# Delta net: V turned by a 16-bit DMA, projections in another order, the output projection's second half in two depths

## The chip, the cores and the metric

One core of a Trainium2 chip runs the whole program. The metric is the device time of one execution in microseconds; lower is better. TensorE (PE), VectorE (DVE), ScalarE (ACT), GpSimd (POOL) and SyncE (SP, which here only issues transfers) run side by side, each through its own list of instructions in order.

## The reference

Two layers on a residual stream of 1024 tokens by 1024 channels: a gated delta net, then chunked attention, each with a gated convolutional feed-forward behind it. The change lies in the first, of 8 heads and 16 chunks of 64 tokens in the reference (the kernel solves 128 tokens at a time).

```python
def gated_deltanet(xn, w_in, conv_w, A_log, dt_bias, out_norm_w, w_out):
    proj = xn @ w_in
    qkv = jax.nn.silu(causal_dwconv(proj[..., :A_CONV_WIDTH], conv_w))
    z = ...; b_raw = ...; a_raw = ...
    q = _l2norm(q) * (A_HEAD_K ** -0.5); k = _l2norm(k); v = qkv[..., 2 * A_QK_WIDTH:]
    beta = jax.nn.sigmoid(b_raw)
    g = -jnp.exp(A_log) * jax.nn.softplus(a_raw + dt_bias)
    o = chunk_gated_delta_rule(q, k, v, beta, g)
    # S_t = exp(g_t) (I - beta_t k_t k_t^T) S_{t-1} + beta_t k_t v_t^T ; o_t = S_t^T q_t
    o = rmsnorm(o, out_norm_w) * jax.nn.silu(z)
    return o.reshape(bsz, seq, A_V_WIDTH) @ w_out

h = h + gated_deltanet(rmsnorm(h, a_norm), ...)
```

## The kernel before, in words

All is kept with channels on the 128 partitions and tokens along them. A product in full precision is three matmuls, of high and low parts (`dense`, L118 to L120): one unit is the three for one block of 128 input channels and 512 tokens, and a tile of 128 output channels and 512 tokens (a half) is eight units. Weights come as `wraw`, ScalarE makes their high part `whi`, GpSimd the low part `wlo` in four slices (L103).

In the delta net, the projections (tiles `acc`) are woven with the heads' small work by a planner, `Flow`. It keeps a clock `T` of its own and a free time per engine, takes the small items that its costs say are ready, by rank, and otherwise one more dense unit; so it writes out the order of PE, DVE and ACT. SP and POOL are ordered by the framework. A list `ORDER` says in which order the projections of K, Q and V of each head come.

A projection's two halves pass `post`: copies out on ACT, the convolution's taps on DVE, then `silu`: a Tanh on ACT and two POOL instructions (L626, L627). V is stored to DRAM as `d_v`, channels by tokens (L630). `prep` loads it for a head and half as `vv` (L761), PE turns it into the PSUM tile `pv` with four transposes (L778), and DVE multiplies it by `sk` back into `vv` (L780). `chain` then walks the chunks: PE products `pc`, DVE and ACT in turns, with `y` written by ACT (L935). `turn` and `turn_last` turn the heads' results for the output projection (L985, L1032), and `split_yt` makes high and low parts of them, `acts`.

The output projection runs tile by tile, first the eight of the first 512 tokens, then the eight of the second (`out_tile`, PSUM tiles `acco`). Each loads one weight tile and the residual as two planes of 16 bits (`xm`), which POOL and DVE weave into `xs` (L1299); DVE adds `xs` to the sum (L1305). A tile of the second half can start when all eight `acts` of that half are there:

```python
wv.dense.append((lambda: True, there("begun", *[("act", k, s) for k in range(KT)]), out_tile(m, s)))
```

The sums of squares for the next norm are gathered after each tile (L357, L359), and when a half is done its normed high and low parts `xh`, `xl` are made (L381 is a low part).

In the attention layer's key and value stage V is already turned through DRAM as 16-bit halves (`turn_halves`, L2201 to L2222, with tiles `vt`, `vu`, `vf`); a similar pair of transfers turns `x` at the start (`xm`, `d_xt`).

## Time and profile before

| | us |
|---|---|
| runs of the kernel: median | 2497.89 |
| runs: lowest, highest | 2497.13, 2501.19 |
| span of the profiled execution | 2493.3 |
| PE, DVE, ACT, POOL busy | 2466.1, 1842.5, 1442.1, 1523.0 |

The profile covers one execution, of which its page gives the span, from the first to the last instruction; what the runs have more lies around the span, and no other time of that execution is listed. A group's row reads: line, engine, operation, what it writes and reads, how often; shortest, median and longest in ns. A row of waits reads: who waited for whom, us in all, times, longest. In a row of the timeline stand the start, the length, the instruction and its count. PE's lengths overlap, so its pace is read from starts.

### The profile page before, as it was taken

How to read it: one execution, taken by the hardware profiler on the slowest of the kernel's cores; microseconds unless marked ns; L12 is line 12 of the kernel's file. 1: busy time of each engine (PE TensorE's matmuls, PEld its weight loads, DVE VectorE, ACT ScalarE, POOL GpSimd, SP SyncE). 2: the span in 40 equal slices, each digit the busy share in tenths (PEclk: the TensorE clock that was granted, in tenths of full speed). 3: DMA queues.
4: the chain of work that ended last, by engine and by line, in shares of the span. 5: the costliest groups of instructions: out<-in, count | busy, mean ns of one | idle time of the engine just before them, and what ended most of it. 6: DMA issues, size and time to landing. Idle time of an engine off the chain costs nothing.

```text
span 2493.3 us, 39279 instructions
## 1 busy us (share of the span) xinstructions
PE 2466.1 (99%) x13785; PEld 2057.0 (83%) x13785; DVE 1842.5 (74%) x2985; ACT 1442.1 (58%) x2770; POOL 1523.0 (61%) x1548
## 2 busy tenths in 40 slices
PE   8999999999999999999999999999999999999998
PEld 6888888888888888888788888888877888888877
DVE  5665874567798888888866656666589788888886
ACT  6444546474465556565555666667456565666555
POOL 3655653357357777777626454455554777778774
PEclk9999999999999999999999999999999999999999
DMA  8734435565347777777841232333444799777788
GB/s 228 188 105 118 142 110 153 156 194 163 96 108 148 150 153 151 153 144 156 183 151 55 67 80 77 81 76 95 145 114 119 184 176 180 166 169 171 152 187 224
DMA packets 383877, 353.19 MB, mean 142 GB/s; under 512 B 97600, under 2 KB 304448, under 8 KB 383680
## 3 DMA queue, kind: packets, MB, share of 16 engines
q1 hardware_dynamic: 350704, 243.46, 34.4%
q0 software_dynamic: 28224, 98.58, 22.5%
q10 hardware_dynamic: 4752, 8.65, 0.9%
q8 instruction: 108, 1.77, 0.3%
q14 instruction: 89, 0.73, 0.1%
HBM read 182.25 MB, written 156.30 MB: 136 GB/s over the span
## 4 chain that ended last, share of the span: by engine, by line
PE 81%; POOL 6%; DVE 4%; issue 4%; DMA 2%; ACT 2%; SPq 0%; ACTq 0%; POOLq 0%; DVEq 0%
PE acc L118 8%; PE pu L1448 8%; PE acc L119 8%; PE acc L120 8%; PE pu L1446 8%; PE pu L1447 8%; PE pd L1448 3%; PE pd L1446 3%; PE pd L1447 3%; POOL ul L1412 3%; PE acco L118 2%; PE acco L120 2%; PE acco L119 2%; PE ptp L2353 2%; PE poT L2399 1%
## 5 line engine op out<-in xcount | busy, mean ns | idle before, releaser
L1412 POOL TENSOR_TENSOR ul<-r,uh 128x512 fp32r<-128x512 f32 x266 | 430.4, 1638 | 258.3 <-ACT uh L1434 253.5
L118 PE MATMUL acc<-xh,whi 128*128 128x512 f32 x896 | 369.3, 413 | 0.5 <-ACT xh L1094 0.5
L119 PE MATMUL acc<-xl,whi 128*128 128x512 f32 x896 | 352.1, 393 | 0.4 <-POOL xl L381 0.3
L120 PE MATMUL acc<-xh,wlo 128*128 128x512 f32 x896 | 351.3, 392 | 0.0
L103 POOL TENSOR_TENSOR wlo<-wraw,whi 128x256 fp32r<-128x256 f32 (+1 forms) x326 | 237.0, 758 | 107.8 <-ACT whi L101 105.3
L1434 ACT CAST uh<-r 128x512 fp32r<-128x512 f32 x289 | 177.1, 623 | 183.3 <-DVE r L1412 148.8
L1448 PE MATMUL pu<-xh,ul 128*128 128x512 f32 x524 | 204.4, 390 | 0.7 <-POOL ul L1412 0.7
L1446 PE MATMUL pu<-xh,uh 128*128 128x512 f32 x524 | 204.4, 390 | 0.7 <-ACT keep L1575 0.7
L1802 ACT COPY stage<-pd 128x1024 f32<-128x1024 f32 x180 | 175.3, 1014 | 49.7 <-PE pd L1448 48.8
L1447 PE MATMUL pu<-xl,uh 128*128 128x512 f32 x524 | 203.9, 389 | 0.0
L120 PEld LDWEIGHTS acc<-xh,wlo 128*128 128x128 f32 x896 | 168.5, 188 | 37.1
L2308 POOL TENSOR_SCALAR sS<-sS,st 128x640 f32<-128x640 f32 (+4 forms) x128 | 87.6, 691 | 178.4 <-DVE st L2306 168.2
L119 PEld LDWEIGHTS acc<-xl,whi 128*128 128x128 f32 x896 | 169.3, 189 | 28.4 <-POOL xl L381 2.5
L118 PEld LDWEIGHTS acc<-xh,whi 128*128 128x128 f32 x896 | 169.1, 189 | 27.5 <-ACT xh L1094 0.9
L1412 POOL TENSOR_TENSOR dl<-a,dh 128x512 fp32r<-128x512 f32 x90 | 153.3, 1703 | 47.4 <-ACT dh L1434 37.2
L1541 DVE SCALAR_TENSOR_TENSOR gate<-gpre,colt,gate 128x1023 f32<-128x1023 f32 (+2 forms) x92 | 176.5, 1919 | 2.5 <-ACT gate L1538 1.8
L1541 DVE SCALAR_TENSOR_TENSOR val<-vpre,colt,val 128x1023 f32<-128x1023 f32 x88 | 149.2, 1696 | 29.3 <-ACT val L1538 29.3
L2298 DVE CUSTOM_DVE_ANT_0 sS<-sc,bt 128x640 f32<-128x640 f32 (+4 forms) x128 | 84.1, 657 | 111.4 <-PE sc L2294 75.9
L1412 DVE TENSOR_TENSOR r<-r,r 128x512 f32<-128x512 f32 x160 | 130.3, 814 | 32.8 <-POOL ul L1412 31.7
L1412 DVE TENSOR_TENSOR el<-val,eh 128x512 fp32r<-128x512 f32 x90 | 85.4, 949 | 43.2 <-ACT eh L1434 43.2
L1448 PEld LDWEIGHTS pu<-xh,ul 128*128 128x128 f32 x524 | 98.4, 188 | 22.8 <-POOL ul L1412 1.4
L1446 PEld LDWEIGHTS pu<-xh,uh 128*128 128x128 f32 x524 | 98.4, 188 | 21.1 <-ACT keep L1575 1.1
(428 smaller groups left out, 7197.9 us busy)
## 6 DMA issues: line engine op xcount, KB each, us to landing
r<-in_f_w_up_dram SPq DMA_DIRECT2D x176, 256.0 KB, 4.5
d_r<-stage POOLq DMA_DIRECT2D x78, 512.0 KB, 8.1
d_c<-stage POOLq DMA_DIRECT2D x70, 512.0 KB, 8.4
a<-in_f_w_down_dram SPq DMA_DIRECT2D x72, 256.0 KB, 2.9
wraw<-in_a_w_in_dram SPq DMA_DIRECT2D x32, 512.0 KB, 4.5
d_e<-stage POOLq DMA_DIRECT2D x32, 512.0 KB, 8.3
wraw<-in_a_w_out_dram SPq DMA_DIRECT2D x16, 512.0 KB, 4.1
d_r<-h ACTq DMA_DIRECT2D x32, 256.0 KB, 2.8
```

Of the source, the lines that this page charges most:

```text
L103: nc.gpsimd.tensor_tensor(lo[:, c], raw[:, c], hi[:, c].bitcast(F32), op=ALU.subtract)
L118: mm(ps, hi[:, kw, wcol : wcol + P], rh[k][s], start=st, stop=False)
L119: mm(ps, hi[:, kw, wcol : wcol + P], rl[k][s], start=False, stop=False)
L120: mm(ps, lo[:, kw, wcol : wcol + P], rh[k][s], start=False, stop=sp)
L1412: tt = lambda eng, o, a, b, op: eng.tensor_tensor(o, a, b, op=op)
L1434: copy(hi, src)
L1446: mm(ps, w[0][:, cw], x[0], start=first, stop=False, skip_group_check=True)
L1447: mm(ps, w[0][:, cw], x[1], start=False, stop=False, skip_group_check=True)
L1448: mm(ps, w[1][:, cw], x[0], start=False, stop=last, skip_group_check=True)
L1541: nc.vector.scalar_tensor_tensor(t_[:, a:c1], p_[:, a - step : c1 - step], w[:, 2 - step : 3 - step], t_[:, a:c1], op0=ALU.mult, op1=ALU.add)
L1802: nc.scalar.copy(t_, ps)
L2308: nc.gpsimd.tensor_scalar(S, S, st[:, 3:4], 1.0, op0=ALU.mult, op1=ALU.mult)
```

## The change

Four things change; the pools' tags for a few small tiles (`tri`, `ba`, `gr`, `nck`, `eg`) change with them, to make room.

1. V is turned by DMA. Behind `silu`, ACT copies V into two planes of 16-bit halves (`cast`, L641), SP stores them in pieces of 128 tokens, and `prep` loads a head and half with a transposing DMA into `vh` (one buffer). ACT copies one plane and POOL the other into `vv` (L788, L789), and DVE multiplies `vv` by `sk` in place. PE no longer takes part.
2. `ORDER` has other places for some of the projections.
3. The second half of the output projection is computed in two passes: `out_deep` takes two output tiles at once, first over input blocks 0 to 3 for all eight tiles, then over blocks 4 to 7. The first pass adds the residual into `h`, the second adds its sum to `h`. A weight load is 4 blocks by 256 columns instead of 8 by 128.
4. The first pass may start when `acts` 0 to 3 of the second half are there, the second when 4 to 7 are.

```diff
-    d_v = [[dram.tile([P, HALF], F32, name=f"d_v{k}_{s}") for s in range(2)] for k in range(KT)]
+    d_v = [[dram.tile([SEQ, P], mybir.dt.uint16, name=f"d_v{k}_{s}") for s in range(2)] for k in range(KT)]
...
+        planes = lambda t_: t_.bitcast(U16).rearrange("p (h t) -> p h t", h=2)
+        woven = lambda t_: t_.bitcast(U16).rearrange("p (t h) -> p h t", h=2)
...
                     t = wv.on("G", 2.0, wv.on("A", 0.66)) + 0.6
+                    if key[0] == "v":
+                        wv.later(t - 0.6, lambda: cast(th))
+                        return
...
+                def cast(th):
+                    nc.scalar.copy(planes(th), woven(d))
+                    nc.sync.dma_start(out=store[s].rearrange("(h b c) t -> c h b t", h=2, b=4), in_=th.bitcast(U16).rearrange("p (h b t) -> p h b t", h=2, b=4))
+                    wv.mark((key[0], key[1], s), wv.on("A", 1.02) + 3.0)
...
-            vv = dp.tile([P, 4, P], F32, name="vv", tag="vv", bufs=4)
-            nc.sync.dma_start(out=vv.rearrange("p c t -> p (c t)"), in_=d_v[hd][s])
+            vh = dq.tile([P, 2, HALF], U16, name="vh", tag="vh")
+            nc.sync.dma_start(out=vh.rearrange("p h t -> p (h t)"), in_=d_v[hd][s], transpose=True)
             t1_ = wv.T + 5.0
...
-            slot = yield from wv.bank()
-            pv = paux.tile([P, HALF], F32, name="pv", tag="pa")
-            for c in range(4):
-                nc.tensor.transpose(pv[:, cs(c)], vv[:, c], ident)
-            wv.pe(4, 0.11)
-            nc.vector.tensor_tensor(vv, pv.rearrange("p (c t) -> p c t", c=4), sk[...].broadcast_to([P, 4, P]), op=ALU.mult)
-            slot[0] = t2_ = wv.on("D", 1.18)
+            vv = dp.tile([P, 4, P], F32, name="vv", tag="vv", bufs=4)
+            w_ = woven(vv.rearrange("p c t -> p (c t)"))
+            nc.scalar.copy(w_[:, 0], vh[:, 0])
+            nc.gpsimd.tensor_copy(w_[:, 1], vh[:, 1])
+            yield max(wv.on("A", 0.78), wv.on("G", 0.93)) - wv.slack
+            nc.vector.tensor_tensor(vv, vv, sk[...].broadcast_to([P, 4, P]), op=ALU.mult)
+            t2_ = wv.on("D", 0.7)
...
+        def out_deep(ms, k0):
+            raw = wp.tile([P, 4, 2 * P], F32, name="wraw", tag="wraw", bufs=2)
+            nc.sync.dma_start(out=raw, in_=a_w_out[k0 * P : (k0 + 4) * P, ms[0] * P : (ms[1] + 1) * P].rearrange("(k p) m -> p k m", p=P))
+            xms = [out_x(m, 1) for m in ms if k0 == 0]
+            yield
+            wt = split_w(raw, [P, 4, 2 * P])
+            wv.on("G", 2.75, wv.on("A", 1.0))
+            yield 4
+            for n, m in enumerate(ms):
+                if k0 == 0:
+                    ps, xs = out_begin(xms[n])
+                else:
+                    ps, xs = pacc.tile([P, HALF], F32, name="acco", tag="acc", bufs=3), h[m][:, hs(1)]
+                for k in range(4):
+                    dense(ps, wt, n * P, *acts, [(k, k0 + k)], 1, first=k == 0, last=k == 3)
+                    if k < 3:
+                        yield
+                if k0 == 0:
+                    nc.vector.tensor_tensor(h[m][:, hs(1)], ps, xs, op=ALU.add)
+                    wv.on("D", 0.64)
+                else:
+                    out_end(m, 1, ps, xs)
+                yield
...
-        ORDER = [... "k2 k0 k1 k3 q2 q0 q1 k5 k4 q3 v0 v1 k6 v2 v3 k7 q4 q5 q6 q7 v5 v4 v6 v7".split()]
+        ORDER = [... "k2 k0 k1 k3 k5 k4 q2 q0 q1 v0 v1 k6 k7 q3 v2 v3 q4 q5 v5 v4 q6 q7 v6 v7".split()]
...
-            for s in range(2):
-                for m in range(KT):
-                    wv.dense.append((lambda: True, there("begun", *[("act", k, s) for k in range(KT)]), out_tile(m, s)))
+            for m in range(KT):
+                wv.dense.append((lambda: True, there("begun", *[("act", k, 0) for k in range(KT)]), out_tile(m, 0)))
+            for k0 in (0, 4):
+                for m in range(0, KT, 2):
+                    wv.dense.append((lambda: True, there(*[("act", k, 1) for k in range(k0, k0 + 4)]), out_deep((m, m + 1), k0)))
```

`out_begin` and `out_end` are the first and last parts of the old `out_tile`: the weaving of `xs`, and the add with the step of the next norm behind it.

The order of PE around the first `prep` of a head (`pqk` is its product of K and Q), before:

```order
L767 MATMUL pqk<-kq 128x128 x4
L118 MATMUL acc<-xh_1_245,whi 128x512
L119 MATMUL acc<-xl_1_246,whi 128x512
L120 MATMUL acc<-xh_1_245,wlo 128x512
L778 MATMUL pv<-ident,vv 128x128 x4
L118 MATMUL acc<-xh_1_249,whi 128x512
```

and now:

```order
L862 MATMUL pm<-D,X 32x32 x32
L778 MATMUL pqk<-kq 128x128 x4
L118 MATMUL acc<-xh_0_253,whi 128x512
L119 MATMUL acc<-xl_0_254,whi 128x512
L120 MATMUL acc<-xh_0_253,wlo 128x512
L118 MATMUL acc<-xh_0_257,whi 128x512
```

The group `pv` is gone from between the units; `pqk` is now L778.

ACT where the first V projections are copied out (L625 or L628 is the Tanh), before:

```order
L610 ACTIVATE u<-acc,colt 128x512
L612 ACTIVATE u<-acc,colt 128x3
L625 ACTIVATE th<-u 128x512
L847 COPY X<-pm 128x256
L689 ACTIVATE E<-E,ngc 128x128 x4
```

and now:

```order
L628 ACTIVATE th<-u 128x512
L641 COPY th<-u 128x1024
L858 COPY X<-pm 128x256
L101 CAST whi<-wraw 128x1024
L641 COPY th<-u 128x1024
L628 ACTIVATE th<-u 128x512
L788 COPY vv<-vh 128x512
```

Copies into planes (L641) and out of `vh` (L788) now stand in ACT's list between a merge's copy `X`, a weight split and the next Tanh.

POOL in the second half of the output projection (`wlo` is a weight split of four slices, `xl` a low part of the normed first half), before:

```order
L1299 COPY xs<-xm 128x512
L103 TENSOR_TENSOR wlo<-wraw,whi 128x256 x4
L1299 COPY xs<-xm 128x512
L381 TENSOR_TENSOR xl_0_7200<-h_1_6584,xh_0_7199 128x512
L103 TENSOR_TENSOR wlo<-wraw,whi 128x256 x4
L1299 COPY xs<-xm 128x512
```

and now:

```order
L1073 TENSOR_TENSOR xl_1_6541<-vv,xh_1_6540 128x512
L1310 COPY xs<-xm 128x512
L103 TENSOR_TENSOR wlo<-wraw,whi 128x256 x4
L1310 COPY xs<-xm 128x512 x2
L103 TENSOR_TENSOR wlo<-wraw,whi 128x256 x4
L1310 COPY xs<-xm 128x512
L381 TENSOR_TENSOR xl_0_7209<-h_1_6608,xh_0_7208 128x512
L1310 COPY xs<-xm 128x512
L381 TENSOR_TENSOR xl_0_7213<-h_3_6610,xh_0_7212 128x512
L103 TENSOR_TENSOR wlo<-wraw,whi 128x256 x4
```

Between two splits stood one copy `xs`, and stand now two, while the first pass runs.

More of the change, by code (lines that the diff above doesn't have):

```diff
@@ L510, in trunk_kernel @@
         dp = ph.enter_context(tc.tile_pool(name="dp", bufs=1, **SB))
-        tri = dp.tile([P, P], F32, name="tri")
+        tri = dp.tile([P, P], F32, name="tri", tag="y0", bufs=2)
         nc.gpsimd.affine_select(out=tri, in_=ones, pattern=[[1, P]], compare_op=ALU.is_ge, fill=0.0, base=0, channel_multiplier=-1)
@@ L522, in trunk_kernel @@
         dq = early_dp.enter_context(tc.tile_pool(name="dq", bufs=1, side="right", **SB))
-        ba = dp.tile([P, 8, 16], F32, name="ba")
+        ba = dp.tile([P, 8, 16], F32, name="ba", tag="S0", bufs=2)
         def gt(name):
@@ L529, in trunk_kernel @@
         beta, gg, t1, t2 = gt("beta"), gt("gg"), gt("t1"), gt("t2")
-        eg, neg_eg, ekd, dec = gt("eg"), gt("neg_eg"), gt("ekd"), gt("dec")
+        neg_eg, ekd, dec = gt("neg_eg"), gt("ekd"), gt("dec")
         gc = dp.tile([P, 2, 8, 8], F32, name="gc")
         gcum, gtot = gc[:, 0], gc[:, 1]
-        gr = dp.tile([64, P], F32, name="gr")
+        gr = dp.tile([P, P], F32, name="gr", tag="S1", bufs=2)[0:64]
         ngc = gt("ngc")
@@ L547, in rsqrt @@
                 nc.vector.scalar_tensor_tensor(y, w, 1.5, y, op0=ALU.add, op1=ALU.mult)
-        ssk, ssq, sk, ck, nck = gt("ssk"), gt("ssq"), gt("sk"), gt("ck"), gt("nck")
+        ssk, ssq, sk, ck, nck = gt("ssk"), gt("ssq"), gt("sk"), gt("ck"), t1
         soo, ff, rr = gg, gt("ff"), gt("rr")
@@ L553, in trunk_kernel @@
         tiles = [0, 0]
+        U16 = mybir.dt.uint16
+        planes = lambda t_: t_.bitcast(U16).rearrange("p (h t) -> p h t", h=2)
+        woven = lambda t_: t_.bitcast(U16).rearrange("p (t h) -> p h t", h=2)
         def units(s, wt, post):
@@ L1153, in gates @@
             nc.sync.dma_start(out=d_g.rearrange("c j t -> (c j) t"), in_=gr)
-            nc.scalar.activation(eg, gcum, AF.Exp)
+            nc.scalar.activation(neg_eg, gcum, AF.Exp)
             nc.scalar.activation(dec, gtot, AF.Exp)
@@ L1157, in gates @@
             nc.scalar.activation(ekd, t2, AF.Exp)
-            nc.vector.tensor_scalar(neg_eg, eg, -1.0, None, op0=ALU.mult)
+            nc.vector.tensor_scalar(neg_eg, neg_eg, -1.0, None, op0=ALU.mult)
             er = dp.tile([64, P], F32, name="er", tag="junk", bufs=1)
@@ L1274, in trunk_kernel @@
         its = {}
-        U16 = mybir.dt.uint16
         d_xt = dram.tile([2 * SEQ, SEQ], U16, name="d_xt")
@@ L1283, in turn_halves, with out_raw, out_x, out_begin @@
             yield wv.T + 6.0
-        def out_tile(m, s):
-            shape = [P, KT, P]
-            raw = wp.tile(shape, F32, name="wraw", tag="wraw", bufs=2)
+        def out_raw(m, s):
+            raw = wp.tile([P, KT, P], F32, name="wraw", tag="wraw", bufs=2)
             nc.sync.dma_start(out=raw, in_=a_w_out[:, m * P : (m + 1) * P].rearrange("(k p) m -> p k m", p=P))
+            return raw, out_x(m, s)
+        def out_x(m, s):
             xm = dp.tile([P, 2, HALF], U16, name="xm", tag="xm", bufs=2)
             nc.sync.dma_start(out=xm, in_=d_xt.rearrange("(c h) t -> c h t", h=2)[m * P : (m + 1) * P, :, hs(s)])
-            yield
-            wt = split_tile(raw)
-            yield 4
+            return xm
+        def out_begin(xm):
             ps = pacc.tile([P, HALF], F32, name="acco", tag="acc", bufs=3)
@@ L1300, in out_tile, with out_end @@
             wv.on("G", 0.60), wv.on("D", 0.6)
-            for k in range(KT):
-                dense(ps, wt, 0, *acts, FULL[k : k + 1], s, first=k == 0, last=k == KT - 1)
-                if k < KT - 1:
-                    yield
+            return ps, xs
+        def out_end(m, s, ps, xs):
             nc.vector.tensor_tensor(h[m][:, hs(s)], ps, xs, op=ALU.add)
@@ L1321, in out_tile, with out_unit @@
             wv.later(wv.on("D", 0.64), then)
+        def out_unit(ps, wt, s, k):
+            dense(ps, wt, 0, *acts, FULL[k : k + 1], s, first=k == 0, last=k == KT - 1)
+        def out_tile(m, s):
+            raw, xm = out_raw(m, s)
             yield
+            wt = split_tile(raw)
+            yield 4
+            ps, xs = out_begin(xm)
+            for k in range(KT):
+                out_unit(ps, wt, s, k)
+                if k < KT - 1:
+                    yield
+            out_end(m, s, ps, xs)
+            yield
[6 more added lines that the diff above has]
+            wv.on("G", 2.75, wv.on("A", 1.0))
+            yield 4
+            for n, m in enumerate(ms):
[6 more added lines that the diff above has]
+                    if k < 3:
+                        yield
+                if k0 == 0:
[3 more added lines that the diff above has]
+                    out_end(m, 1, ps, xs)
+                yield
         def tail(it):
@@ L1328, in trunk_kernel @@
         env["cut"] = 4
-        ORDER = [(w[0], int(w[1])) for w in "k2 k0 k1 k3 q2 q0 q1 k5 k4 q3 v0 v1 k6 v2 v3 k7 q4 q5 q6 q7 v5 v4 v6 v7".split()]
+        ORDER = [(w[0], int(w[1])) for w in "k2 k0 k1 k3 k5 k4 q2 q0 q1 v0 v1 k6 k7 q3 v2 v3 q4 q5 v5 v4 q6 q7 v6 v7".split()]
         wv = Flow()
```

2 lines of the change are left out of this document (1 added, 1 removed).

## The prediction

> **What bounds the kernel now.** I read the page's busy shares first, then the stage that the change touches as one window, then what TensorE waited for inside it. The columns of the window are TensorE's matmuls, its weight loads, VectorE, ScalarE, GpSimd, the granted clock and the DMA.
>
> ```profile
> span 2493.3 us, 39279 instructions
> ...
> PE 2466.1 (99%) x13785; PEld 2057.0 (83%) x13785; DVE 1842.5 (74%) x2985; ACT 1442.1 (58%) x2770; POOL 1523.0 (61%) x1548
> ...
> core 0: us, PE busy (x) PEld busy (x) DVE busy (x) ACT busy (x) POOL busy (x), PEclk, DMA share, GB/s
> 20.00:640.00 620.00, 619.57 (x5012) 520.38 (x5010) 394.09 (x1015) 328.26 (x876) 341.46 (x450) 1.00 0.53 151
> ...
> PE po L985 <- DVE mn L724: 0.2, 1, 0.2
> PE pv L778 <- DMA vv<-d_v: 0.2, 1, 0.2
> ```
>
> From 20 to 640 us, which is the delta net from its second projection to the end of its output projection, PE is idle for 0.43 us and two waits account for it. The clock is 1.00 throughout. So this stage lasts as long as PE's own work: a change gains what PE work it takes out, and loses what PE waits it puts in. Nothing that only shortens another engine can gain more than 0.43 us here.
>
> **The V transposes leave PE.** Per head and half, four transposes of `vv` into `pv` go (L778), 64 in all. What four cost is read from one such place; columns are start, length, instruction.
>
> ```profile
> 172.56 0.39 PE L120 MATMUL acc<-xh,wlo 128*128 128x512 f32 x1
> 172.78 0.60 PE L778 MATMUL pv<-ident,vv 128*128 128x128 f32 x4
> 173.14 0.48 PE L118 MATMUL acc<-xh,whi 128*128 128x512 f32 x1
> 173.46 0.40 PE L119 MATMUL acc<-xl,whi 128*128 128x512 f32 x1
> 173.69 0.40 PE L120 MATMUL acc<-xh,wlo 128*128 128x512 f32 x1
> ...
> L778 PE MATMUL pv<-ident,vv x64: 270/273/329, 172.8 to 538.8; 128*128 128x128 f32 x64
> ```
>
> A lone 512-column matmul starts 0.23 after the one before (173.46 to 173.69); lengths overlap and don't add up. From 172.56 to 173.46 are 0.90, where two pitches would take 0.46: the group costs 0.44, 0.08 of it on the matmul behind it. Sixteen groups: 16 x 0.44 = 7.0. Counting the starts alone (0.36 a group) gives 5.8; I take 7.0, because the delayed neighbour is in the rows too. No other matmul is added or dropped: the order of the program differs by these 64 alone. The new weave meets small groups at other places; at 0.08 a meeting, 16 more or fewer are 1.3, so this term ends at 4.5 and 8.3.
>
> **What V costs elsewhere.** The key-value stage already does the same thing, so most prices are there: a ScalarE copy into planes (`vt`), a store in pieces, a transposing load (`vu`), a copy back (`vf`). The rows are of the views by tile: shortest, median and longest in ns; a landing line belongs to the transfers above it.
>
> ```profile
> L2229 ACT COPY vt<-acc x14: 1012/1012/1012, 1377.3 to 1717.6; 128x1024 uint16<-128x1024 uint16 x14
> DMA to landing us min/median/max: 2.6/2.6/5.4
> ...
> L2212 ACT COPY vf<-vu x28: 755/779/796, 1391.7 to 1740.2; 128x512 uint16<-128x512 uint16 x28
> L2206 SPq DMA_TRANSPOSE vu<-d_vt x14: 1160/1171/2198, 1380.9 to 1730.7; - x14
> DMA to landing us min/median/max: 2.9/3.5/4.7
> ...
> L761 SPq DMA_DIRECT2D vv<-d_v x16: 319/332/892, 161.7 to 524.1; - x16
> DMA to landing us min/median/max: 2.0/3.2/7.2
> ...
> L1299 POOL COPY xs<-xm x16: 758/926/1242, 541.1 to 634.5; 128x512 uint16<-128x512 uint16 x16
> L780 DVE TENSOR_TENSOR vv<-pv,sk x16: 652/691/692, 173.5 to 539.1; 128x512 f32<-128x512 f32 x16
> L1049 DVE TENSOR_TENSOR spare<-spare x12: 644/689/1597, 512.5 to 549.3; 128x512 f32<-128x512 f32 x12
> ```
>
> ScalarE gets 16 x (1.01 + 0.78) = 28.6, on 328.26 busy of 620. GpSimd gets 16 x 0.93 = 14.9, on 341.46. SP's queue gets 16 x (1.17 - 0.33) = 13.4. VectorE's product by `sk` stays at 0.69 from SBUF. All of it lies beside PE and I cost it at nothing. The cover is the distance in PE's order: from the last matmul of a V projection's first half to the first product that reads this `vv`, heads 0 to 3 have 72, 63, 99 and 93 long matmuls between them before, and 129, 111, 162 and 147 after. The 57 more of head 0 are 13 us at 0.23. The path grows by far less: the copy (1.01), the slower issue and landing (1.17 + 3.5 against 0.33 + 3.2), and copy and product (0.93 + 0.69) where transposes and product stood (0.44 + 0.69): 2.7 together. The store lands in 2.6 or up to 5.4, against 2.0 to 7.2 over the old stores and loads; no loss there.
>
> The waits that it adds: ScalarE's plane copy waits for GpSimd's last step of SiLU, its copy back waits for the transposed load, and behind both stand the chain's `y` copies, which PE waits for. `th` (tag `zt`, three buffers, shared with the gates and `yo`) is now held until the store lands, so a later Tanh can wait 2.6 for it. On SP, the transposed load waits for its store and for the one `vh` buffer, with weight loads behind it. What such a wait has cost so far:
>
> ```profile
> ACT u L610 <- POOL u L627: 4.8, 3, 2.6
> ...
> DVE T L841 <- DMA D<-d_u: 4.4, 1, 4.4
> DVE h L1305 <- POOL wlo L103: 15.4, 6, 4.5
> ```
>
> ScalarE already waited for GpSimd up to 2.6 and VectorE for a DMA once 4.4, in the window where PE stood 0.43 in all. The weave holds waits of that size, so I take 0 for the new ones; the far bounds are those of the rivals.
>
> **The other order of projections** moves K ahead of Q and each V one or two tiles. The same 22 tiles run; with 0.43 idle it can gain at most that: 0.
>
> **The output projection's second half.** PE does the same 192 matmuls. Each of 8 tiles is closed twice, so VectorE adds 8 x 0.69 (the length of L780, the same size) = 5.5, beside PE. Weight loads stay 8 of the same size. What the split buys is lateness: from the last head's transposes (L1032) to the first matmul that needs its result there are 39 long matmuls before and 129 after. But PE doesn't wait there now, so this gains 0. What is late next is GpSimd: in the first four pairs eight `xs` copies fall on four weight splits, where eight tiles had eight of each.
>
> ```profile
> 583.50 0.39 PE L118 MATMUL acco<-xh,whi 128*128 128x512 f32 x1
> ...
> 584.18 0.39 PE L118 MATMUL acco<-xh,whi 128*128 128x512 f32 x1
> ...
> 608.85 2.84 POOL L103 TENSOR_TENSOR wlo<-wraw,whi 128x256 fp32r<-128x256 f32 x4
> 611.61 1.02 POOL L1299 COPY xs<-xm 128x512 uint16<-128x512 uint16 x1
> 613.37 1.30 POOL L381 TENSOR_TENSOR xl<-h,xh 128x512 fp32r<-128x512 f32 x1 [0.74 <-ACT xh L393]
> 614.63 3.48 POOL L103 TENSOR_TENSOR wlo<-wraw,whi 128x256 fp32r<-128x256 f32 x4
> 618.06 1.75 POOL L381 TENSOR_TENSOR xl<-h,xh 128x512 fp32r<-128x512 f32 x1
> ...
> 588.00:612.00 24.00, 20.88 (x25) 1.00 0.55 172
> ```
>
> The last row is GpSimd alone: 20.88 busy of 24. A unit of three matmuls takes 0.68 (583.50 to 584.18), so 32 units are 21.8 of PE. In them GpSimd owes 4 splits (mean 3.16) + 8 copies (0.93) + 3 `xl` (1.30; they stand there in its new order) = 24.0. With the shortest rows it is 4 x 2.84 + 8 x 0.76 + 3.9 = 21.3, with the longest 4 x 3.48 + 8 x 1.24 + 3 x 1.75 = 29.1. So PE waits for a `wlo` by between 0 and 7.3. A split starts half a pair (2.7) ahead and PE needs its slices one by one, which absorbs most of the mean excess of 2.2; I take 0.8.
>
> **Sum.** -7.0 + 0 + 0 + 0.8 = -6.2. The profiled span is 2493.3; the runs' median is 2497.89, so 4.6 lie around the span and stay. 2497.89 - 6.2 = 2491.7.
>
> **Rivals.** (a) GpSimd eats the gain: at its longest rows 7.3 of wait, less the half pair of 2.7 that a split is ahead, leave 4.6: -7.0 + 4.6 = -2.4, 2495.5, within 0.2% (5.0 us, about what can be told from no change). For it: VectorE's 15.4 of waits on GpSimd in just this place. Against it: none of them reached PE. The same result comes from 2 us of scattered new waits.
>
> (b) Slower: ScalarE's queue. The planner lets 5.0 pass from the load's issue to the copy back. The rows give 1.17 + 3.5 = 4.7, but at worst 2.2 + 4.7 = 6.9. If all 16 copies back stood 1.9 and PE with them, that is 30.4: -7.0 + 30.4, 2521.3. It decides, at 5.0 above the median, from 0.75 a copy ((7.0 + 5.0) / 16). Against it stand the 2.6 that did not reach PE and the longer distances.
>
> (c) Slower: the product of two SBUF tiles. L780, with one operand in PSUM, never took over 692 ns; L1049, with both in SBUF, took up to 1597. If GpSimd holds up all 16 so, and PE with them, it is 16 x 0.906 = 14.5: 2497.89 - 7.0 + 14.5 = 2505.4. It decides from the same 0.75 each. Against it: L1049's median is 689. [...]
>
> [...]
>
> **How the numbers follow.** The forecast (-5 to -9, the bound of 8.3 and some spread) gets 0.60, (a) 0.29, (b) 0.08, (c) 0.03. Faster is the first, same is (a), slower is (b) and (c). The range leaves out the slow ones and little else: its low end is -8.3 with a microsecond of the median's own spread, 2488.5; its high end is (a) with 4 us more of waits, 2499.5. The likeliest case alone spans 2488.9 to 2492.9.
>
> **What would show it.** Right: no `pv` in the trace, PE idle in the stage still under 2, the last `acco` matmul 6 to 8 earlier, ScalarE some 29 busier and GpSimd some 15. (a) would show as PE waits on POOL wlo near the `acco` tiles, (b) as ACT waits on DMA `vh` or POOL `u` with PE waits on ACT `y`, (c) as a long DVE product with PE waiting on DVE `vv`. Wrong altogether: PE idle over 5 in the stage.

## The result: slower by 0.6%, with PE waits that were not there before

| | us |
|---|---|
| changed kernel: median of 4 runs (lowest, highest) | 2513.84 (2510.04, 2517.44) |
| kernel before, on the same chip: median | 2497.65 |
| ratio, 95% interval | 1.0058 [1.0045, 1.0072] |
| profiled execution: time, span | 2510.04, 2508.3 |

Medians and ratios leave out one run each of e2 and e3, which took 4984.20 and 3055.89 us.

The forecast was 2491.7 in a range to 2499.5. What lies around the span is 1.7 us here (2510.04 - 2508.3), so of the 4.6 in the prediction's sum some 2.9 would be the spread between executions; the forecast does not depend on it. The first two lines are from the page of the changed kernel; the row with 620.00 is the stage as one window (columns as before: TensorE, its weight loads, VectorE, ScalarE, GpSimd, clock, DMA). In the changed kernel's code lines are numbered anew: L723 was L712, L765 was L754, L941 was L930.

```profile
span 2508.3 us, 39147 instructions
...
PE 2466.2 (98%) x13721; PEld 2052.1 (82%) x13721; DVE 1850.4 (74%) x2993; ACT 1469.4 (59%) x2802; POOL 1538.8 (61%) x1564
...
20.00:640.00 620.00, 606.25 (x4892) 504.35 (x4891) 397.24 (x1013) 349.46 (x900) 347.31 (x455) 0.99 0.56 148
...
PE pg L723 <- ACT ke L765: 4.6, 1, 4.6
PE acco L120 <- POOL wlo L103: 4.0, 4, 2.3
PE pu L1497 <- ACT uh L1485: 1.7, 1, 1.7
PE pu L914 <- ACT vv L917: 1.3, 1, 1.3
PE pc L941 <- DVE vv L791: 1.3, 2, 1.1
PE pc L937 <- DVE S L956: 1.1, 2, 0.7
```

Span less PE's busy time was 27.2 (2493.3 - 2466.1) and is 42.1: 14.9 more, the whole growth of the span (15.0). PE has 64 instructions fewer and yet the same busy time: the clock records show 0.5 for 6.8 us from 254.8 and for 3.4 us from 661.0, and there long matmuls start 0.43 apart (259.73 to 260.16), where at 1.00 they start 0.23 apart (262.00 to 262.23). In the stage PE stands 13.75 of 620 where it stood 0.43. The last six rows are the largest waits of PE between 20 and 680 us: no one engine, and not one of these was there before.

Where the 15.0 us are lost can be read from the starts of four matmuls in the two timelines. The last matmul of the projections starts 1.7 later (541.51, now 543.17). The stretch from there to the first of the output projection (542.11, now 549.14) adds 5.4, the output projection itself (its last at 643.01, now 655.03) 5.0, and all that comes behind it 3.0.

PE's largest wait, link by link. The rows are of the timeline, of SP, ScalarE and PE around 252 us, with the idle time and its releaser in brackets:

```profile
249.34 0.38 SPq L574 DMA_DIRECT2D wraw<-in_a_w_in_dram  x1
249.81 2.78 SPq L1001 DMA_DIRECT2D d_y<-yo  x2
252.68 0.39 SPq L642 DMA_DIRECT2D d_v<-th  x1
...
246.05 1.05 ACT L641 COPY th<-u 128x1024 uint16<-128x1024 uint16 x1
255.29 0.63 ACT L628 ACTIVATE th<-u 128x512 f32<-128x512 f32 x1 [8.19 <-DMA d_y<-yo]
255.82 1.12 ACT L765 ACTIVATE ke<-pk,ekd 128x128 f32<-128x128 f32 x4
...
252.03 0.40 PE L120 MATMUL acc<-xh,wlo 128*128 128x512 f32 x1
257.00 1.22 PE L723 MATMUL pg<-kq 128*128 128x128 f32 x4 [4.57 <-ACT ke L765]
```

Tanh (L628) needs one of the three `zt` buffers. One is held by V's planes (L641) until their store has gone, two by `yo`, whose stores (L1001) stand on SP behind a weight load (L574). That load waits for a weight buffer, the last 5.2 us of it for GpSimd's split `wlo`. So ScalarE stands 8.19, its `ke` behind that comes late, and PE stands 4.57.

### The profile page after: what moved, and what is told of

Read it like the earlier page. It is cut to its first block, busy times and chain, and to the rows that moved or that the text cites. A ratio compares the mean times of both kernels' runs of the same rounds, so it can differ in the third digit from the quotient of the medians.

```text
span 2508.3 us, 39147 instructions
## 1 busy us (share of the span) xinstructions
PE 2466.2 (98%) x13721; PEld 2052.1 (82%) x13721; DVE 1850.4 (74%) x2993; ACT 1469.4 (59%) x2802; POOL 1538.8 (61%) x1564
## 3 DMA queue, kind: packets, MB, share of 16 engines
q0 software_dynamic: 28224, 98.58, 22.2%
q8 instruction: 108, 1.77, 0.3%
## 4 chain that ended last, share of the span: by engine, by line
PE 69%; POOL 6%; DVE 5%; issue 5%; ACT 3%; DMA 2%; ACTq 0%; POOLq 0%; DVEq 0%; SPq 0%
PE pu L1499 8%; PE pu L1497 8%; PE pu L1498 8%; PE acc L118 5%; PE acc L119 5%; PE acc L120 5%; PE pd L1498 3%; PE pd L1499 3%; PE pd L1497 3%; POOL ul L1463 2%; PE ptp L2404 2%; PE acco L120 2%; PE acco L118 2%; PE acco L119 2%; PE poT L2450 1%
```

## Experiments

All of e1 to e18 ran in comparison with the kernel before on the same chip; "ratio" is to that. 0.001 is 2.5 us.

### The first stall alone, and the parts alone (e1 to e4)

**e1**: one line of the changed kernel.

```diff
-            nc.sync.dma_start(out=d_y[k][s], in_=yo)
+            nc.scalar.dma_start(out=d_y[k][s], in_=yo)
```

> The changed kernel, with one edit: the store of `yo` goes out on ScalarE's queue, behind the copy that wrote it, and no longer on SP's queue, where it stood behind a weight load that waited for GpSimd. Nothing else moves. Theory A (one buffer: V's planes keep a `zt` buffer until their store has landed, the stores of `yo` are late on SP, so a Tanh waits 8.2 us, TensorE waits 4.6 for `ke` and then runs 6.8 us at half clock): the wait of Tanh on the store of `yo` is gone, PE's 4.6 and the half clock near 255 us with it, and the time falls by 6 to 9 from the changed kernel's, to 1.0020 to 1.0035 of the kernel before. Theory B (the output projection in two depths keeps GpSimd busy and its late weight splits carry the loss), C (the other order of projections carries it) and D (the late transposed load, spread over the heads) all expect no more than 2 us from this edit: 1.005 to 1.006.

Measured: 2510.12, ratio 1.0044 [1.0032, 1.0056]. In the trace the 8.2 on `yo` and PE's 4.6 on `ke` are gone, no half clock follows, and the last unit of the projections starts 1.97 earlier than in the kernel before, where it was 1.77 later: 3.7 won there. By the ratios it is 3.5 us, with overlapping intervals, where theory A expected 6 to 9; at the end of the two profiled spans it is 0.1. Of the 3.7, 2.4 are lost again by the end of the output projection: a wait for `wlo` near 554 us is as long as in the changed kernel but now drew a half clock of 3.4 us, and one for `whi` ahead of it is new (1.0). So theory A names the link rightly, but the stall is one of several, and its length is not what its removal gains.

**e2, e3, e4**: V by DMA alone (old ORDER and `out_tile`); the two depths alone on the kernel before; the new ORDER alone on the kernel before.

> V's turn by DMA alone, with the old order of projections and the old output projection. The prediction's term for it was -7.0. Theory A: the buffer conflict belongs to this part, so Tanh waits on stores of `yo` here too, wherever V projections and `turn` now meet; with one such stall of 5 to 8 us the time comes out at 0 to +3 from the kernel before (1.0000 to 1.0012), with none of them at -5 to -7. Theories B and C: this part brings its -7.0, 0.9972. Theory D: VectorE's products by `sk` stand and TensorE waits for `vv` at several heads; +2 or more (from 1.0008), with the waits spread.

> The output projection's second half in two depths alone, on the kernel before. The prediction's term for it was +0.8, between 0 and 7.3. Theory B: this is where the loss lies, +6 to +12 (1.0024 to 1.0048), with PE waiting on GpSimd's `wlo` between 600 and 640 us. Theories A, C and D: +1 to +4 (1.0004 to 1.0016), since the changed kernel's waits on `wlo` in this stretch add up to some 3 us.

> The other order of projections alone, on the kernel before. The prediction's term was 0. Theory C: the planner packs the small work worse in this order, +6 or more (from 1.0024), with PE waits between 240 and 560 us. Theories A, B and D: within 2 us of the kernel before (0.9992 to 1.0008).

Measured: e2 2520.56, 1.0084 [1.0071, 1.0097]; e3 2505.28, 1.0022 [1.0012, 1.0032]; e4 2520.37, 1.0084 [1.0071, 1.0097]. V by DMA alone costs 21 us and ORDER alone 21, and all three parts together 14.5: the first two belong together, and either alone is worse than both. No theory had this. In the traces of e2 and e4 most of it lies between the last `acc` matmul of a projection and the first `acco` of the output projection: the first `acco` starts 20.3 and 14.7 later than before, the last one 26.0 and 22.2. That stretch as one window, in the kernel before:

```profile
541.51:542.11 0.60, 0.60 (x7) 0.55 (x5) 0.60 (x1) 0.60 (x2) 0.60 (x2) 1.00 0.86 96
```

In the changed kernel:

```profile
543.17:549.14 5.97, 4.24 (x34) 3.82 (x33) 4.65 (x7) 3.79 (x10) 4.84 (x5) 1.00 0.95 317
```

In e2, V by DMA alone:

```profile
525.30:562.40 37.10, 28.31 (x375) 25.14 (x373) 23.94 (x53) 29.59 (x78) 19.19 (x18) 0.77 0.82 206
```

And in e4, the order alone:

```profile
540.62:556.76 16.14, 12.19 (x158) 10.88 (x157) 8.63 (x16) 10.52 (x26) 4.60 (x6) 0.82 0.63 196
```

Before, 4 small matmuls lie between the two, and the stretch lasts 0.60 us. After, it is 32 and 5.97; in e2 372 and 37.10; in e4 156 and 16.14. There PE has only the heads' small products, which take their inputs from VectorE and ScalarE, and no long matmul to put between; in e2 it is busy for 28.31 of 37.10 at a mean clock of 0.77. V by DMA makes a head's preparation longer: from the issue of V's load to the product by `sk` the 16 `prep`, which are taken one at a time, need 254.9 in all before and 308.6 in e2. It also makes PE's own work shorter. That the long matmuls therefore run out before the heads are done, and that the new order makes up for it by feeding the heads earlier, fits e2 and the pair, but was not tested by itself, and it does not say why the order alone (e4) has a gap. The counts can be read from the order of the instructions before any run.

Of the 12.5 us that e3's profiled span is longer, 6.2 lie between the first and the last matmul of the output projection, and 5.0 ahead of it:

```profile
PE acco L120 <- POOL wlo L103: 4.1, 3, 2.4
PE pm L862 <- issue: 2.3, 1, 2.3
```

The second row is a PE wait near 531 us, with a half clock of 3.4 us behind it, at an instruction that the split does not touch. The profile shows no cause for it.

### The same on top of each other, and a stall by hand (e5 to e8)

**e5** is the changed kernel again; **e6** the changed kernel with the old loop over `out_tile(m, s)` for both halves; **e7** e1 with, in the first pass, both planes of `xs` on VectorE:

```diff
-                (nc.gpsimd, nc.vector)[i].tensor_copy(hm[:, :, i], xm[:, i])
+                (nc.vector, nc.vector)[i].tensor_copy(hm[:, :, i], xm[:, i])
```

> The changed kernel once more, as the base for the three kernels beside it on the same chip: 1.0045 to 1.0072 of the kernel before, and in its trace the stall near 253 us with the half clock behind it.

> The changed kernel without the two depths: V by DMA and the new order of projections, and the old output projection in 16 tiles of eight units. Theory B2 (the two depths cost here what they cost alone, some 6 us, by late weight splits): 4 to 7 us less than the changed kernel. Theory E (the long matmuls run out before the heads' small work is done, and the two depths give PE something to fill this with): no gain, or up to 3 us more than the changed kernel, with more small matmuls standing alone between the last projection and the first output tile. Theory A (the buffer of Tanh) expects the stall near 253 us unchanged. On V by DMA and ORDER: alone they gave +22 and +21 us. If they only work as a pair, this kernel is far below either, at +8 or so from the kernel before.

> The changed kernel with `yo`'s store on ScalarE's queue (as in e1_yo_act) and, in the first pass over the depth, both planes of `xs` copied by VectorE, so that GpSimd's weight splits no longer stand behind copies that wait for `xm`. Theory B2 (GpSimd's queue holds up the splits): the waits of PE on `wlo` between 600 and 640 us go, and the time is 2 to 4 us under e1_yo_act's, 2506 to 2508. Rival: the splits are late by their own length and by their weight loads; less than 1 us, 2509 to 2511.

Measured: e5 2513.57, 1.0067 [1.0054, 1.0080]; e6 2513.77, 1.0058 [1.0046, 1.0070]; e7 2512.13, 1.0060 [1.0046, 1.0075]. Taking the two depths out changes nothing that can be told, so theory B2 falls for the changed kernel: what PE waits there, it waits for a `wlo` or a `whi` with either loop. V by DMA with the new order (e6) is as slow without the depths as with them, and has the same 32 matmuls alone in the gap; against e2 the order has won 6.5 us by the ratios. e7 takes GpSimd's copies away; PE's waits on `wlo` from 560 to 655 us go from 1.9 (e1) to 0.9, but 0.9 more is waited for ScalarE's `whi`, and the time does not fall. The rival holds.

**e8**: four stalls written into the kernel before, in the second half's tiles 1, 3, 5 and 7.

```diff
+                if s == 1 and k == 1 and m in STALLS:   # {1: 4, 3: 6, 5: 8, 7: 13}
...
+                    nc.tensor.transpose(pz[:, 0:P], ident, ident)
...
+                    for _ in range(STALLS[m]):
+                        nc.scalar.copy(dm[:, 0:P], pz[:, 0:P])
+                    nc.tensor.transpose(pz[:, P : 2 * P], dm[:, 0:P], ident)
```

> The kernel before with four stalls of PE put in by hand, in tiles 1, 3, 5 and 7 of the second half of the output projection: ScalarE copies a 128x128 piece of PSUM 4, 6, 8 and 13 times, and PE transposes the result. By a copy's 0.27 us and some 0.5 for the two hand-overs PE stands 1.6, 2.1, 2.7 and 4.0, in all 10.4. Theory F (a stall costs more than its length: behind one of 2 us and more the granted clock is 0.5 for 3.4 or 6.8 us): clock 0.5 behind the last three, 1.7 to 3.4 lost behind each, in all +14 to +19 (1.0056 to 1.0076). Rival (the clock's drops in the traces have another cause): clock 1.00 throughout, +10 to +11 (1.0040 to 1.0044).

Measured: 2517.24, 1.0070 [1.0058, 1.0082], some 17 us. PE waits 10.4 in the four (1.55, 2.06, 2.64, 4.13); the rest is the clock, a 2.25 wait at the same place near 531 us as in e3, and a stall at the feed-forward's start (its cause is under e9). The clock's records change only at multiples of 3.41 us from each other: in the changed kernel at 254.82, 261.65, 661.01 and 664.42. The windows below are cut at that grid: the window of a stall and the one behind it, for the second, the third (which lies across two windows) and the fourth stall.

```profile
620.99:624.40 3.41, 1.35 (x8) 0.84 (x7) 3.40 (x5) 2.30 (x8) 3.41 (x4) 1.00 0.39 121
624.40:627.81 3.41, 3.41 (x9) 2.73 (x10) 0.69 (x1) 1.80 (x3) 2.58 (x4) 0.50 0.61 186
634.64:638.05 3.41, 2.59 (x12) 1.84 (x11) 2.17 (x3) 1.05 (x3) 2.28 (x3) 1.00 0.15 43
638.05:641.46 3.41, 1.59 (x8) 1.35 (x9) 0.00 (x0) 2.54 (x7) 0.62 (x1) 1.00 1.02 328
641.46:644.88 3.42, 3.42 (x17) 2.83 (x16) 0.49 (x1) 0.00 (x0) 2.21 (x4) 1.00 0.07 21
...
651.70:655.11 3.41, 0.00 (x0) 0.00 (x0) 0.83 (x1) 3.03 (x13) 0.28 (x1) 1.00 0.11 42
655.11:658.52 3.41, 3.19 (x8) 2.60 (x9) 0.00 (x0) 0.17 (x1) 0.00 (x0) 0.50 0.00 0
```

2.06 in one window brought the half clock, 2.64 cut into 0.82 and 1.82 did not. For these stalls theory F holds in this form: what counted was PE's idle share of one window, not the stall's length.

### Taking the named waits away, and filling the gap (e9 to e11)

**e9**: e1, V's store on ScalarE's queue as well, and the last three squares of the second half's norm in other buffers.

```diff
-            sq = acc if k == 0 else env["tmp"]()
+            sq = acc if k == 0 else env["last" if k > 4 and s == 1 and "last" in env else "tmp"]()
...
+        env["last"] = lambda: dp.tile([P, HALF], F32, name="sq", tag="at", bufs=4)
```

> The changed kernel with three edits of where things wait, none of work: the stores of `yo` and of V go out on ScalarE's queue, behind the copies that write them, instead of on SP's queue; and the last three squares of the second half's norm (`sq`) lie in the buffers of `at` instead of those of `zt`. Theory A (buffers and queues): no stall near 253 us (4 and some 3 of half clock); SP no longer waits for ScalarE's plane copy (26 us in all); and the load of the feed-forward's first weights, which lies where the last `sq` lay, no longer waits for that `sq`, so the stall near 661 us (1.8 and 1.7 to 3.4 of half clock) goes. In all 7 to 11 us under the changed kernel, 1.0015 to 1.0035 of the kernel before. Rival (the stalls only move on, as with e1_yo_act, where 3.9 us gained near 255 us left about 3 at the end): 3 to 6 under the changed kernel, 1.0035 to 1.0055.

Measured: 2513.89, 1.0058 [1.0046, 1.0071]: no gain, less even than the rival allowed. The stalls near 253 and 661 us are gone; others came, of up to 2.6 us, at places where PE had not waited (PE for VectorE's `U` at 172 us, for ScalarE's `yo` at 252, for GpSimd's `kq` at 267). One of the three edits is confirmed by itself, that of the squares: e14, which keeps it and puts the stores back on SP, has no stall near 661 us either. The load of the feed-forward's weights goes to memory where the three `zt` buffers were; in the built programs the last `sq` lies in the lowest of them in the changed kernel, e4, e8 and e12, and not in the kernel before, e2, e3 and e9. SP's wait for the step that frees it, in the waits of SP of the kernel before:

```profile
SPq L1492 <- DVE nacc L364: 0.7, 1, 0.7
```

And in the changed kernel, with ScalarE's step for which PE then waits:

```profile
SPq L1543 <- DVE nacc L364: 14.6, 1, 14.6
...
660.89 0.62 ACT L1485 CAST uh<-r 128x512 fp32r<-128x512 f32 x1 [3.70 <-DMA r<-in_f_w_up_dram]
```

All four of the first group have this stall (1.7 to 2.0 us of PE, and a half clock behind it), none of the second.

**e10**: e2 with two dummy weight tiles, 32 units, behind the last projection.

> e2_turn_only (V by DMA alone, 1.0084) with work added: behind the last projection two more weight tiles are loaded, split and multiplied, 32 units of three long matmuls, whose sums nobody reads. A unit takes 0.68 to 0.69 us, so this is 22 us more of PE's own work. Theory E (in e2_turn_only the long matmuls run out 37 us before the output projection may begin, and PE waits through the heads' small products with nothing between): the added units fall into this stretch and cost little; +0 to +8 on e2_turn_only, 1.0085 to 1.0117. Rival (PE is the bound there and the stretch was no waiting): +22, 1.0172.

Measured: 2521.23, 1.0092 [1.0078, 1.0106], against 1.0084 for e2: 22 us of matmuls cost 2 by the ratios and nothing by the medians. The same stretch, now with them:

```profile
525.40:570.79 45.39, 44.79 (x488) 38.61 (x487) 29.58 (x59) 33.85 (x96) 25.52 (x26) 1.00 0.71 196
```

PE is busy for 44.79 of 45.39 at full clock. The stretch is 8.3 longer with 22 us more in it, so some 14 of its 37.1 had been waiting and half clock, and the rest the small matmuls themselves; most of the 8.3 is won back in the output projection behind it, whose last matmul starts only 0.6 later than in e2. Theory E is shown for V by DMA alone.

**e11**: e9 with an order in which the planner's clock finds no gap.

> e9_fixes with another order of the projections: k2 k0 k5 q2 k1 k3 k4 q0 q1 v1 k6 k7 v0 q3 v2 v3 q4 v5 v4 q6 q5 q7 v6 v7. The planner's own clock counts 0.4 us in which it found nothing to place, against 4.0 in the changed kernel's order. Theory E: the small matmuls that stand alone between the last projection and the first output tile go, and with them the waits of PE near 547 and 559 us (1.4 to 2.5 and 2.3, with 1.7 of half clock at times); 4 to 8 us under e9_fixes, 0.998 to 1.001 of the kernel before. Rival (the planner's clock doesn't know the queues and buffers, and each new order brings stalls of its own, 10 to 20 us as in every order tried so far): no better than e9_fixes, 1.002 to 1.006.

Measured: 2507.46, 1.0037 [1.0024, 1.0051], 5 us under e9 (the intervals overlap a little). Two small matmuls are left between the last projection and the first output tile, in 0.37 us. So the gap went as theory E said, but the time is where the rival put it, still 9 us above the kernel before.

### Is it V by DMA, or any new order? (e12 to e15)

**e12** and **e13** swap two neighbours of ORDER in the kernel before (k6 with v1; q7 with v5).

> The kernel before with two neighbours of ORDER swapped (k6 ahead of v1). The planner's own clock ends at the same 587.1 and finds nothing to place in the same 2.6 us. Theory G (the order before is one in which the waits of the other engines do not reach PE, and a new order of the same work brings stalls of its own): +4 or more (from 1.0016), with new PE waits in the stage. Theory H (the stalls come from V by DMA; an order as good by the planner is as good on the chip): within 2 us but for one thing: the last `sq` lies in the lowest of the three `zt` buffers here, where the feed-forward's first weights go, which should bring the stall of 1.8 us at the start of that stage with 1.7 to 3.4 of half clock; so +2 to +4 (1.0008 to 1.0016), all of it there.

> The kernel before with q7 and v5 swapped in ORDER. The planner's own clock ends at 584.9, 2.2 us earlier, with 0.4 us of nothing to place; the last `sq` lies in the highest `zt` buffer, as before, so no stall at the feed-forward's start. Theory G: slower than before, +2 to +15, by new PE waits. Theory H: 0 to -2 (0.9992 to 1.0000).

Measured: e12 2503.23, 1.0016 [1.0007, 1.0025]; e13 2501.51, 1.0010 [1.0001, 1.0019]. e12 loses 3.9 of its profile's 6.3 from the feed-forward's start on, with the stall that its `sq` foretold, and has a PE wait of 1.2 at 531 us; e13 has one of 2.0 at 405 us. Both waits are of the kind for which the profile shows no cause. e12 fits the ranges of both theories; e13 lies in that of theory G and not in that of H. So even an order that leaves no gap costs 2 to 4 us, in part by waits of PE that theory H does not have, but not 9 to 15: most of that comes with V by DMA, or with an order that leaves a gap (e4).

**e14**: e11 with the stores back on SP; **e15**: e14 without the two depths.

> e11_order_a with the stores of `yo` and of V on SP's queue again; the order without the gap and the place of the last three `sq` stay. If the stores on ScalarE's queue brought the waits of e11 (PE on copies of ScalarE at 239, 248 and 256 us): 3 to 6 us under e11, 2501 to 2505. If theory A's conflict comes back instead (V's planes hold a `zt` buffer while SP's queue stands): a Tanh waits for a store and the time is e11's or above, 2507 to 2514.

> e14_order_sq with the old output projection in place of the two depths. In e6 this made no difference, with PE's gap ahead of it. Here, without the gap: theory B2 (the two depths cost some 4 us by late weight splits, as alone in e3): 2 to 5 us under e14. Rival (they only change which weight is late): within 2 us of e14.

Measured: e14 2509.05, 1.0042 [1.0029, 1.0054]; e15 2508.37, 1.0033 [1.0021, 1.0044]. Neither edit tells; in e14 a Tanh does wait for V's store, but 2.2 us and once. Its trace shows another link that I had under V's price. GpSimd and PE near 253 us, SP ahead of 399 us and PE there:

```profile
244.84 1.30 POOL L783 TENSOR_TENSOR kq<-kq,eq 128x512 f32<-128x512 f32 x1
253.18 0.76 POOL L789 COPY vv<-vh 128x512 uint16<-128x512 uint16 x1 [7.03 <-DMA vh<-d_v]
253.87 0.62 POOL L629 TENSOR_SCALAR th<-th 128x512 f32<-128x512 f32 x1
254.57 1.72 POOL L630 TENSOR_TENSOR kq<-kq,th 128x512 f32<-128x512 f32 x1
...
256.35 0.90 PE L666 MATMUL pq<-ident,kq 128*128 128x128 f32 x3 [3.31 <-POOL kq L630]
...
388.41 5.26 SPq L772 DMA_TRANSPOSE vh<-d_v  x1
393.79 0.51 SPq L693 DMA_DIRECT2D E<-d_g  x1
394.35 0.50 SPq L741 DMA_DIRECT2D d_m<-cm  x1
394.94 1.57 SPq L678 DMA_DIRECT2D kq<-d_kq  x1
...
402.66 1.09 PE L666 MATMUL pq<-ident,kq 128*128 128x128 f32 x4 [3.54 <-DMA kq<-d_kq]
```

GpSimd's copy of one plane stands 7.03 on the transposed load, the SiLU behind it is late, and PE stands 3.31. At 388 us the issue of a transposed load itself holds SP for 5.26, and PE stands 3.54 for the load of `kq` that is issued behind it.

### The planner's prices, and GpSimd out of the path (e16 to e18)

**e16** and **e17**: e14 with longer prices for three transfers and an order found for each.

```diff
-            t1_ = wv.T + 5.0
+            t1_ = wv.T + 7.0
...
-            wv.mark(("in", hd), wv.T + 5.5)
+            wv.mark(("in", hd), wv.T + 8.5)
...
-                    wv.mark((key[0], key[1], s), wv.on("A", 1.02) + 3.0)
+                    wv.mark((key[0], key[1], s), wv.on("A", 1.02) + 4.5)
```

> e14_order_sq with three prices of the planner set to what the traces show: 7.0 instead of 5.0 from the issue of the transposed load to the copy back (issue 1.17 and landing 5.0 in the middle, up to 8.8), 8.5 instead of 5.5 for the load of `kq` (it stands on SP behind V's transfers), 4.5 instead of 3.0 for V's store. The order is one found for these prices: k2 k0 v1 q2 k5 k4 q0 k1 k3 q1 k7 v0 k6 q3 v2 v3 q5 q4 v4 v5 q6 q7 v6 v7; the planner counts 6.0 us of nothing to place (13.6 in e14's order at these prices). Theory I (the stalls are where the planner's prices are too short): PE's waits on `kq` and on `vv` go, the planner's own gap of 6 stays; 2500 to 2505, 1.001 to 1.003. Rival (queues and buffers that the planner has no model of): no better than e14, 1.004.

> The same three prices with another order: k2 k0 k3 k1 k5 q1 q2 q0 v0 k4 k6 k7 v3 v1 v2 q4 q3 q5 v5 v4 v6 q6 q7 v7, 6.2 us of nothing to place. Theory I: as e16, 2500 to 2505. Rival: the two orders differ by more than 3 us from each other, with stalls in other places.

Measured: e16 2514.23, 1.0065 [1.0050, 1.0080]; e17 2514.91, 1.0065 [1.0052, 1.0079]. Theory I falls. With longer prices the planner holds the heads' work back, and the gap is back: 164 and 300 small matmuls between the last projection and the first output tile, in 16.7 and 21.5 us.

**e18**: e14 with the second plane copied by VectorE.

```diff
-            nc.gpsimd.tensor_copy(w_[:, 1], vh[:, 1])
             yield max(wv.on("A", 0.78), wv.on("G", 0.93)) - wv.slack
+            nc.vector.tensor_copy(w_[:, 1], vh[:, 1])
```

> e14_order_sq with one edit: the second plane of V is copied by VectorE, just ahead of the product by `sk`, and no longer by GpSimd; the order of PE and ScalarE is the same. Theory D (GpSimd takes its instructions in order, its copy stands on the transposed load, 48 us in all in e14, and SiLU and weight splits behind it reach PE late): GpSimd's wait on that load is gone, and PE's 3.3 on GpSimd's `kq` near 253 us with its half clock (1.7); the wait near 399 us, which comes over SP's queue, stays; 3 to 6 us under e14, 2503 to 2506. Rival (VectorE stands on the load instead, and the chain's steps behind it reach PE late): within 2 us of e14, with PE waits on VectorE in place of those on GpSimd.

Measured: 2503.21, 1.0018 [1.0009, 1.0027], 6 us under e14 by the ratios, and the intervals do not touch. GpSimd's waits for the transposed load in e14 (us in all, times, longest):

```profile
POOL vv L789 <- DMA vh<-d_v: 47.8, 11, 9.2
```

In e18, PE's largest waits from 20 to 640 us, and who waited for the transposed load:

```profile
PE pq L666 <- DMA kq<-d_kq: 3.3, 1, 3.3
PE acco L120 <- POOL wlo L103: 2.8, 4, 1.5
...
ACT vv L788: 4.8, 1
DVE vv L790: 1.1, 1
```

PE's 3.3 on GpSimd's `kq` is gone, the 3.3 on the load of `kq` over SP is left. VectorE does not stand in GpSimd's place: it waits 1.1 once, and ScalarE 4.8 once, where GpSimd, which came to its copy early, waited 47.8. Theory D is shown in this order of the program. No version beat the kernel before; of those with V by DMA this is the nearest. GpSimd's copy was not moved in the changed kernel itself.

## Why the prediction was wrong, step by step

**"This stage lasts as long as PE's own work."** Right for the kernel before; it was then used as if it held after any change. The sign that the prediction itself set, "PE idle over 5 in the stage", came true with 13.75. The last `acco` matmul, foretold 6 to 8 earlier, starts 12.0 later.

**Transposes, -7.0.** The 64 matmuls are gone, but what that won is not shown. In the profile of the changed kernel the idle time grew by 14.9 and the half clocks (6.8 + 3.4 us) took at most 5.1, together 20.0, and the span grew by 15.0: 5.0 were won. The same sum for e2 is 18.8 + 15.4 - 28.1 = 6.1. Both lie within 4.5 to 8.3, but the other profiles with V by DMA give anything from -0.3 (e11) to 8.0 (e16), so the sum can't tell 7.0 from less.

**V on the other engines.** The amounts were right: ScalarE +27.3 (28.6 foretold), GpSimd +15.8 (14.9). The landing was not. The row `vu` gave 2.9/3.5/4.7, the new rows are these:

```profile
L772 SPq DMA_TRANSPOSE vh<-d_v x16: 1159/1168/2255, 153.2 to 536.8; - x16
...
POOL vv L789: 29.0, 7
...
DMA to landing us min/median/max: 3.1/5.0/6.8
...
L791 DVE TENSOR_TENSOR vv<-vv,sk x16: 649/686/1530, 170.2 to 548.5; 128x512 f32<-128x512 f32 x16
```

5.0 in the middle instead of 3.5, and GpSimd stands 29.0 us for it in all. V's old load landed in 3.7. A landing is counted from the start of the issue, so the prediction's 1.17 + 3.5 counts the issue twice: by its own rows the path grows by 1.8 and not 2.7, and the worst landing in (b) is 4.7 and not 6.9. The reckoning of distances ("2.7 together" against 57 more long matmuls) covered V's own path to PE, and PE hardly waited for V's own product (1.3 on `vv` L791). It did not cover what stands behind the waiting copy on GpSimd and behind the issue on SP.

**"The weave holds waits of that size, so I take 0 for the new ones"**: the step that failed. It put nothing for them; PE stood 13.75 in the stage instead of 0.43, with a half clock of 6.8 us behind the largest stall. The very wait that cost most was named there, a later Tanh for a `zt` buffer because V's planes hold one, and priced by the store's landing, 2.6. It was 8.2, because the release of the next buffer, that of `yo`, stood in SP's queue behind a weight load that waited for a buffer of its own. And a wait of 2.6 that did not reach PE at its old place says nothing of another place: what hides it is the row of long matmuls behind it (in e10, with 22 us of them put in, PE stands 0.60 of 45.39, where it stood 8.79 of 37.10 in e2).

**ORDER, 0.** That it "can gain at most that", the 0.43 of idle time, bounded one side only. Alone the order costs 21 us (e4). (It has 24 tiles, not 22.) The places looked at were V's path for the first four heads and the last head's way to the output projection's second half; the end of the projections, where 4 small matmuls became 32, was not.

**The two depths, 0 and 0.8.** In place the size was about right: with and without them no difference can be told (e5 and e6, e14 and e15). Alone they cost 5.5 (e3), within the 7.3 of the upper bound for the wait, and the profile has a stall in it that the split does not explain.

**The rivals.** (a) came in small part: PE waited 4.0 for `wlo`, its sign, but 2.3 of that near 559 us, ahead of the two depths, where e6 has the same wait without them; 1.7 are left in the second half, against 0.8. (b) had the load and the wrong engine: ScalarE's copies hardly waited for it, GpSimd's did, and in e14's order one such copy was enough for a stall of 3.3 and a half clock. (c) seems to have come once. Of the 16 products eleven took 0.65 to 0.69 and five 0.80 to 1.53, 1.9 more in all where 14.5 had been priced, and PE stood behind the longest:

```profile
400.58 2.50 POOL L986 TENSOR_TENSOR vv<-vv,rr 128x512 f32<-128x512 f32 x2 [0.92 <-DVE rr L547]
402.10 1.53 DVE L791 TENSOR_TENSOR vv<-vv,sk 128x512 f32<-128x512 f32 x1
403.69 0.49 PE L941 MATMUL pc<-vv,U 128*128 128x128 f32 x2 [1.06 <-DVE vv L791]
```

GpSimd runs beside it for 0.98, as (c) has it, and PE stands 1.06, the sign that the prediction named. In the kernel before, the five of the twelve `spare` products (L1049) with GpSimd at work beside them took 0.75 to 1.60, the seven others 0.64 to 0.69. Here it is at work beside all five long products, but also beside six of the eleven short ones, at 441.31 for the whole 0.69. That GpSimd is what made a product long was not tested.

On V's store, where the prediction saw "no loss": its 3.2 mixes V's old stores and loads. The old stores alone landed in 2.0/2.8/4.4, V's new ones, in pieces of 128 tokens, in 2.6/3.8/6.9, while the stores of `kq`, whose pieces did not change, went from 3.4 to 3.7 in the middle. So V's stores did get slower by up to 1.0 in the middle; that it is the pieces was not tested.

**What stays open.** The waits of 1.2 to 2.3 us at `pm` matmuls near 531 us (e3, e8, e12) and 405 us (e13), which end with no releaser in the profile and are not in the kernel before. And how the changed kernel's six stalls of over 1 us add up when taken away at once: e9 took two away and won nothing. So the waits are shown in the traces, and three links to them by an edit each (e1 for `yo`, e9 and e14 for the squares, e18 for GpSimd's copy, the last in another order), but no run shows how much of the 14.5 each of them carries.

## What to carry to other kernels

When PE is the bound because every other engine's waits are covered by long matmuls, count in the order of the instructions how many of those stand behind each wait after the change, above all where one stage's long work ends and the next one's may not start: a stretch of small dependent matmuls is paid with all its waits (8.79 of 37.10 in e2), and 22 us of long ones to fill it cost 2 (e10). Price a new hold on a shared buffer by the queue in which its release stands (8.19 here), not by the transfer's landing (2.6); and price a late load by what stands behind it on each engine that takes its instructions in order, which a copy on the engine that needs the result anyway can avoid (waits of 47.8 for the load in e14, of 4.8 and 1.1 in e18). Taking one stall away moves the rest of the weave, so its length is not what is won (in e1 3.7 at that place, 0.1 at the end of the span).

## What the hardware showed that was not expected

A stall of PE can cost more than its length, by how it falls: behind the 4.57 near 253 us the changed kernel's clock is at 0.50 for 6.83 us. The clock's drops start on a grid of 3.41 us whose phase differs from run to run (254.82 and 661.01 in the changed kernel, 624.40 and 655.11 in e8). Counted over the 17 profiles whose clock drops before the end, from 16 us, where the clock's records begin, at full clock: each of the 30 grid windows in which PE stood 1.87 us or more was followed by a window at half clock, 8 of the 39 with 1.1 to 1.87, and 2 of the 164 with 0.6 to 1.1. Eight of these last ten lie at the start of the feed-forward, between 650 and 670 us, so the idle share of one window does not settle every case. The changed kernel's largest stall as such windows:

```profile
251.40:254.81 3.41, 1.03 (x6) 0.55 (x5) 2.11 (x4) 0.00 (x0) 0.00 (x0) 1.00 0.96 306
254.81:258.22 3.41, 1.22 (x5) 1.22 (x6) 0.00 (x0) 2.93 (x10) 2.13 (x3) 0.50 0.27 62
258.22:261.63 3.41, 3.41 (x12) 2.83 (x11) 2.27 (x15) 3.41 (x7) 1.61 (x2) 0.50 0.61 189
261.63:265.04 3.41, 3.41 (x17) 2.75 (x16) 2.86 (x6) 1.49 (x3) 3.33 (x5) 1.00 0.56 120
```

PE is busy for 1.03 of the first window and 1.22 of the second, and the window behind each of these runs at 0.50. By the count, a window with PE busy for up to 1.5 of its 3.41 us was enough each time.

The issue of V's transposing load held SP for 1.17 us in the middle (1.18 in e14 and e18), for 3.7 once in e18 and for 5.26 once in e14.
